# A top-k search on two engines: one engine's tiles given to the scheduler first, and a mask operation moved from ScalarE to VectorE

## The chip, the core and the metric

The kernel runs on one core of a Trainium2 chip. The core has five instruction streams that run side by side and in order: TensorE (PE, matrix products), VectorE (DVE), ScalarE (ACT), GpSimd (POOL) and SyncE (SP), which here only issues DMA transfers. The metric is the device time of one execution, in microseconds; lower is better.

## The reference, cut to what matters

One transformer layer over 1024 tokens of width 1024. After a norm, one projection of the input feeds four token mixers: a convolution (A), differential attention (B), stick-breaking attention (C) and sparse attention (D). Their results are gated, merged and projected, and a gated feed-forward layer follows. The part that matters here is the key selection of D:

```python
logits = einsum('bqhd,bkd->bqhk', qi[:, t0:t1], ki[:, :kl]) * IDX_HD ** -0.5
score = einsum('bqhk,bqh->bqk', relu(logits), wi[:, t0:t1])
score = where(arange(kl) <= qpos, score, -inf)
_, idx = top_k(score, 256)
...
s = einsum('bqhd,bqkd->bqhk', q[:, t0:t1], k[idx]) * scale
p = softmax(where(valid, s, -inf))
```

For each of the 1024 query rows the 256 best scored keys are kept, and the attention runs over these alone. The kernel does it with a mask: it finds the value of the 256th best score of each row, and adds 0 to the attention scores of the chosen keys and -1e30 to the others.

## The kernel before, in words

Rows are handled in tiles of 128 (`t` is 0 to 7; tile `t` has `(t+1)*128` keys). Tiles 0 and 1 have at most 256 keys and need no search. The scores of tiles 2 to 7 lie side by side in one SBUF tile, `score`; `sct(t)` is the part of tile `t`.

The 256th best value is found bit by bit, in two halves: 15 bits of the upper 16 bits of the score (into `T1`), then 16 bits of the lower half among the keys whose upper half is equal (into `T2`). In each round, each tile counts how many keys reach the trial value, and the bit is kept or not. VectorE does tiles 7, 6, 3 and 2 (`V_T`, `search_v`, lines 609 to 619): one count for each tile (L605, scratch output `junkb`) and three small operations on all four (L614, L617, L618). ScalarE does tiles 5 and 4 (`A_T`, `search_a`, lines 621 to 636): three operations for each tile and round (L632, L633, L634), and L636 at the end.

Between the halves lies a step on VectorE for every tile (lines 650 to 659): a count of the keys above `T1` (L605), a test for equality (L654, scratch output `eqb`), a product that puts the lower halves of the scores into the keys (L657). At its end the wanted rank `kreq` is lowered by the counts (L659), and from it ScalarE's search gets `kq` (L625, L626). After both halves, lines 662 to 666 join the halves into the value `Tx`, and lines 668 to 678 make the mask of each tile, `t` = 2 to 7: a count (L605), an equality (L672), a running sum (L673), a comparison (L675), an addition (L677), all on VectorE, and last the mask itself, on ScalarE:

```python
A.activation(sct(t), keyt(t), AF.Identity, scale=-NEG, bias=negc)
```

Attention D starts at line 684. It takes tile 7 first (line 697). Its first VectorE operation, L708, adds the mask `sct(7)` to the scores of the keys, which TensorE has made (L466).

The instructions are written in program order and given to a scheduler, which lays them out on a timeline that it estimates: on each engine, of the instructions that it takes to be ready, the one that stands first in the program goes first. What comes out is a fixed stream for each engine. On the chip an instruction that waits holds up all that stand behind it in its engine's stream.

A tile pool hands out its buffers by tag. The scratch outputs `junkb` and `eqb` of VectorE's part come from one pool, `radj`, with one buffer and one tag:

```python
with pool("rad", 1) as rad, pool("radj", 1) as radj, pool("rada", 1) as rada:
...
def count(dst, src, t, scal, op):
    j = radj.tile([P, S], BF, name="junkb", tag="j")
```

ScalarE's scratch (`junka`) has a pool of its own, `rada`.

Around the search stand projections, which come before it in the program. Each (`proj`, line 356) loads a weight tile by DMA (`wraw`, line 181), splits it into a rounded part on ScalarE (`whi`, L184) and a rest, mostly on GpSimd (`wlo`, L185), and multiplies it in 48 TensorE instructions (L365). Results leave through ScalarE (L524 for plain tiles; L534, L535 and GpSimd's L536 for `qc` and `kc`; L397, L398, L402, L406 and GpSimd's L403, L404, L405, L407 for tiles with rotary positions) and are stored by DMA in `qk_s`. The gate projections (`gate_tile`, line 542) come after all attention in the program. The products of the modulation (`adaps` L202, `adae` L211, `adac` L214) pass through ScalarE too.

Of the kernel before, what the change touches and what calls it, by code (L numbers as in the profile page):

```python
# [12 lines left out]
BF = mybir.dt.bfloat16  # L13
I32 = mybir.dt.int32
U16 = mybir.dt.uint16
I16 = mybir.dt.int16
AF = mybir.ActivationFunctionType
OP = mybir.AluOpType
# [4 lines left out]
S = 1024  # L23
D = 1024
P = 128
# [6 lines left out]
NEG = -1.0e30  # L32
# [62 lines left out]
V_T = [7, 6, 3, 2]  # L95
A_T = [5, 4]
NV = len(V_T)


def kc(t):  # L100

    return V_T.index(t) if t in V_T else NV + A_T.index(t)
# [10 lines left out]
def tile_hybrid_block(ctx, tc, x, pos, ada, pk, cst, w_in, w_br, w_out, w_up, w_dn, out):  # L113
# [6 lines left out]
    V, G, A, PE = nc.vector, nc.gpsimd, nc.scalar, nc.tensor  # L120
# [28 lines left out]
    epsc, halfpi, onec, negc = zcol[:, 0:1], zcol[:, 1:2], zcol[:, 2:3], zcol[:, 4:5]  # L149
# [119 lines left out]
    with ExitStack() as mix:  # L269
# [11 lines left out]
        with pool("xtp", 1) as xtp, pool("adp", 8) as adp:  # L281
# [4 lines left out]
            for t in range(NT):  # L286
                xt = adp.tile([P, D], F32, name="xt", tag="w")
                dma(xt, x[t * P:(t + 1) * P, :])
                if t == 0:
# [9 lines left out]
                                op0=OP.mult, op1=OP.add)  # L299
# [15 lines left out]
            for m in range(4):  # L315
                mod_affine(m, A1, B1, "g1", pmm, "mm", stp, "st", adp)
                for j in (2 * m, 2 * m + 1):
                    V.tensor_scalar(out=xT[:, j, :], in0=xT[:, j, :], scalar1=A1[:, j:j + 1],
                                    scalar2=B1[:, j:j + 1], op0=OP.mult, op1=OP.add)
                    A.copy(hH[:, j, :], xT[:, j, :])  # L320
                    V.tensor_tensor(out=hL[:, j, :], in0=xT[:, j, :], in1=hH[:, j, :].bitcast(F32),  # L321
                                    op=OP.subtract)
# [3 lines left out]
            for kind in ("inv16", "inv32"):  # L326
# [4 lines left out]
                                op0=OP.mult, op1=OP.add)  # L331
                V.tensor_scalar(out=kk, in0=kk, scalar1=MAGIC, scalar2=None, op0=OP.subtract)
                for c in (_C1, _C2, _C3):
                    V.scalar_tensor_tensor(out=ang, in0=kk, scalar=-float(c), in1=ang,
                                           op0=OP.mult, op1=OP.add)
                V.tensor_scalar(out=ang, in0=ang, scalar1=3.1415925, scalar2=-3.1415925,
                                op0=OP.min, op1=OP.max)
# [9 lines left out]
        for i in range(2):  # L347
            V.tensor_tensor(out=lamt, in0=pc("lam", 64 * i, 64 * i + 32), in1=pc("lam", 64 * i + 32, 64 * i + 64),
                            op=OP.mult)
# [105 lines left out]
        NB = NT - 2  # L455
        off = [0]
# [32 lines left out]
        with pool("scp", 1) as scp, ExitStack() as scx:  # L489
            score = scp.tile([P, NTOT], F32, name="score")  # L490
            sct = lambda t: score[:, off[t - 2]:off[t - 1]]
            with pool("iqk", 4) as iqk, pool("itm", 3) as itm:
# [5 lines left out]
                for h in range(8):  # L498
# [3 lines left out]
                    for t in range(2, NT):  # L502
                        n = (t + 1) * P
# [4 lines left out]
                        if h == 0:  # L508
                            V.tensor_scalar(out=sct(t), in0=tmp[:, :n], scalar1=wiT[:, t, h:h + 1],
                                            scalar2=zcol[:, 3:4], op0=OP.mult, op1=OP.add)  # L510
                        else:
                            V.scalar_tensor_tensor(out=sct(t), in0=tmp[:, :n], scalar=wiT[:, t, h:h + 1],
                                                   in1=sct(t), op0=OP.mult, op1=OP.add)
# [71 lines left out]
            with pool("rad", 1) as rad, pool("radj", 1) as radj, pool("rada", 1) as rada:  # L585
                key = rad.tile([P, NTOT], BF, name="key")
                keyt = lambda t: key[:, off[t - 2]:off[t - 1]]
                cnt = rad.tile([P, NB], F32, name="cnt")
                ge = rad.tile([P, NB], F32, name="ge")
                sg_ = rad.tile([P, NB], F32, name="sg_")  # L590
                kreq = rad.tile([P, NB], F32, name="kreq")
                Ti = rad.tile([P, 2, NB], I32, name="Ti")
                T1 = rad.tile([P, NB], F32, name="T1")
                T2 = rad.tile([P, NB], F32, name="T2")
# [7 lines left out]
                def count(dst, src, t, scal, op):  # L602
                    j = radj.tile([P, S], BF, name="junkb", tag="j")
                    n = (t + 1) * P
                    V.tensor_scalar(out=j[:, :n], in0=src, scalar1=scal, scalar2=None, op0=op, op1=OP.add,  # L605
                                    accum_out=dst[:, kc(t):kc(t) + 1])
                    return j

                def search_v(T, dt, bits):

                    v = slice(0, NV)
                    V.memset(T[:, v], 0.0)
                    for b in range(bits - 1, -1, -1):
                        V.tensor_scalar(out=cf[:, v], in0=T[:, v], scalar1=float(1 << b), scalar2=None, op0=OP.add)  # L614
                        for t in V_T:
                            count(cnt, keyt(t).bitcast(dt), t, cf[:, kc(t):kc(t) + 1], OP.is_ge)
                        V.tensor_tensor(out=ge[:, v], in0=cnt[:, v], in1=kreq[:, v], op=OP.is_ge)  # L617
                        V.scalar_tensor_tensor(out=T[:, v], in0=ge[:, v], scalar=float(1 << b), in1=T[:, v],  # L618
                                               op0=OP.mult, op1=OP.add)

                def search_a(T, dt, bits):

                    a = slice(NV, NB)
                    V.memset(Bn[:, a], 0.5 - float(1 << (bits - 1)))
                    V.tensor_tensor(out=kq[:, a], in0=pc("nn", NV), in1=kreq[:, a], op=OP.subtract)  # L625
                    V.tensor_tensor(out=kq[:, a], in0=kq[:, a], in1=kreq[:, a], op=OP.subtract)  # L626
                    for b in range(bits - 1, -1, -1):
                        for t in A_T:
                            k = slice(kc(t), kc(t) + 1)
                            n = (t + 1) * P  # L630
                            j = rada.tile([P, S], BF, name="junka", tag="j")
                            A.activation(j[:, :n], keyt(t).bitcast(dt), AF.Sign, bias=Bn[:, k], accum_out=sgs[:, k])  # L632
                            A.activation(sgn[:, k], sgs[:, k], AF.Sign, bias=kq[:, k])  # L633
                            A.activation(Bn[:, k], sgn[:, k], AF.Identity, bias=Bn[:, k],  # L634
                                         scale=-0.5 * float(1 << b))
                    A.activation(T[:, a], Bn[:, a], AF.Copy, scale=-1.0)  # L636
# [7 lines left out]
                for t in A_T + V_T:  # L644
                    c = off[t - 2]
                    V.tensor_scalar(out=keyt(t), in0=score.bitcast(BF)[:, 2 * c + 1:2 * off[t - 1]:2],
                                    scalar1=sg_[:, kc(t):kc(t) + 1], scalar2=None, op0=OP.mult)
                search_a(T1, I16, 15)
                search_v(T1, I16, 15)
                for t in A_T + V_T:  # L650
                    count(cnt, keyt(t).bitcast(I16), t, T1[:, kc(t):kc(t) + 1], OP.is_gt)
                    e = radj.tile([P, S], BF, name="eqb", tag="j")
                    n = (t + 1) * P
                    V.tensor_scalar(out=e[:, :n], in0=keyt(t).bitcast(I16), scalar1=T1[:, kc(t):kc(t) + 1],  # L654
                                    scalar2=None, op0=OP.is_equal)
                    c = off[t - 2]
                    V.tensor_tensor(out=keyt(t).bitcast(U16), in0=score.bitcast(U16)[:, 2 * c:2 * off[t - 1]:2],  # L657
                                    in1=e[:, :n], op=OP.mult)
                V.tensor_tensor(out=kreq, in0=kreq, in1=cnt, op=OP.subtract)  # L659
                search_a(T2, U16, 16)  # L660
                search_v(T2, U16, 16)
                V.tensor_copy(Ti[:, 0, :], T1)
                V.tensor_copy(Ti[:, 1, :], T2)
                V.scalar_tensor_tensor(out=Ti[:, 0, :], in0=Ti[:, 0, :], scalar=16, in1=Ti[:, 1, :],
# [3 lines left out]
                for t in range(2, NT):  # L668
                    n = (t + 1) * P
                    tx = Tx[:, kc(t):kc(t) + 1]  # L670
                    g_ = count(cnt, sct(t), t, tx, OP.is_gt)
                    V.tensor_scalar(out=keyt(t), in0=sct(t), scalar1=tx, scalar2=None, op0=OP.is_equal)  # L672
                    V.tensor_tensor_scan(out=sct(t), data0=ones[:, 0:1].to_broadcast([P, n]), data1=keyt(t),  # L673
                                         initial=cnt[:, kc(t):kc(t) + 1], op0=OP.mult, op1=OP.add)
                    V.scalar_tensor_tensor(out=keyt(t), in0=sct(t), scalar=float(TOPK), in1=keyt(t),  # L675
                                           op0=OP.is_le, op1=OP.mult)
                    V.tensor_tensor(out=keyt(t), in0=keyt(t), in1=g_[:, :n], op=OP.add)  # L677
                    A.activation(sct(t), keyt(t), AF.Identity, scale=-NEG, bias=negc)

            adx.close()  # L680

# [466 lines left out]
```

## Time and profile before

| | us |
|---|---|
| median of 3 runs | 2032.14 |
| lowest and highest run | 2029.38, 2036.47 |
| the profiled execution | 2032.69 |
| its span, first to last instruction | 2030.9 |
| busy in it: TensorE, VectorE, ScalarE, GpSimd | 1855.4, 1154.4, 829.5, 472.9 |

The rows in the section below come from the profiled execution; their times are in us from the start of its span. 1.8 us of its time lie outside the span. "Busy" counts instructions in execution; a matrix product that runs at a lower clock is busy for longer. "Granted clock" is the share of TensorE's full clock of 2.4 GHz that it was given; its lower level of 1.2 GHz reads as 0.5.

### The profile page before, as it was taken

The page shows a single profiled execution, that of the slowest core. Times are in us where ns is not written, and L with a number is a line of the kernel's source. Part 1 is how long each engine was busy: PE and PEld are TensorE (multiplying, and loading weights), DVE is VectorE, ACT ScalarE, POOL GpSimd, SP SyncE. Part 2 cuts the span into 40 slices and gives each one's busy share as a digit, 9 for nine tenths or more (in the row PEclk, how much of TensorE's full clock was granted, in tenths as well). Part 3 has the DMA queues.
Part 4 walks back from the last instruction along what each step waited for, and adds up shares of the span by engine and source line. Part 5 has one row for each costly group of instructions (what it writes and reads, how often), then busy time and mean ns, then how long its engine had stood idle before and what let it go on. Part 6 is the DMA issues. An engine that isn't in the chain of part 4 may idle for free. (4 is left out here: it accounts for less than half of the span.)

```text
span 2030.9 us, 22858 instructions
## 1 busy us (share of the span) xinstructions
PE 1855.4 (91%) x8792; PEld 1443.3 (71%) x8792; DVE 1154.4 (57%) x1731; ACT 829.5 (41%) x1458; POOL 472.9 (23%) x244
## 2 busy tenths in 40 slices
PE   6888877499999999899999899999999999999996
PEld 3655555376767776677787668788888888888875
DVE  6759999605899857685113765532343334433457
ACT  5556666236545645463222444333122212221122
POOL 0102145272111110011205610222122212222024
PEclk9988989699999999899999999999999999999999
DMA  8364423444514242513113632121111101111114
GB/s 312 94 165 151 174 84 93 126 92 104 187 57 125 78 129 69 147 42 115 62 63 129 225 122 83 63 73 42 32 63 58 47 32 52 62 52 42 32 62 145
DMA packets 61038, 197.30 MB, mean 97 GB/s; under 512 B 9153, under 2 KB 9281, under 8 KB 60929
## 3 DMA queue, kind: packets, MB, share of 16 engines
q1 hardware_dynamic: 60928, 195.84, 30.6%
q8 instruction: 69, 1.13, 0.2%
q14 instruction: 41, 0.33, 0.1%
HBM read 154.13 MB, written 41.68 MB: 96 GB/s over the span
## 5 line engine op out<-in xcount | busy, mean ns | idle before, releaser
L185 POOL TENSOR_TENSOR wlo<-wraw,whi 128x1024 fp32r<-128x1024 f32 x126 | 317.4, 2521 | 1384.2 <-ACT whi L184 1348.2
L365 PE MATMUL mm<-hH,whi 128*128 128x512 f32 x864 | 353.5, 409 | 49.6 <-ACT whi L184 31.5
L365 PE MATMUL mm<-hH,wlo 128*128 128x512 f32 x864 | 350.4, 406 | 3.7 <-POOL wlo L185 3.7
L365 PE MATMUL mm<-hL,whi 128*128 128x512 f32 x864 | 351.9, 407 | 0.9 <-DVE hL L321 0.9
L184 ACT CAST whi<-wraw 128x1024 fp32r<-128x1024 f32 x144 | 150.6, 1049 | 413.2 <-PE ups L1017 283.7
L1017 PE MATMUL ups<-h2h,whi 128*128 128x512 f32 x704 | 277.6, 395 | 1.3 <-DVE h2h L994 1.3
L1017 PE MATMUL ups<-h2l,whi 128*128 128x512 f32 x704 | 277.5, 394 | 0.5 <-DVE h2l L995 0.5
L1017 PE MATMUL ups<-h2h,wlo 128*128 128x512 f32 x704 | 274.5, 390 | 0.0
L1022 DVE SCALAR_TENSOR_TENSOR u<-ups,pkt,u 128x1023 f32<-128x1023 f32 x44 | 56.4, 1283 | 350.8 <-ACT u L1021 350.8
L365 PEld LDWEIGHTS mm<-hH,whi 128*128 128x128 f32 x864 | 166.6, 193 | 95.6 <-ACT whi L184 32.0
L365 PEld LDWEIGHTS mm<-hH,wlo 128*128 128x128 f32 x864 | 166.5, 193 | 41.4 <-POOL wlo L185 4.8
L365 PEld LDWEIGHTS mm<-hL,whi 128*128 128x128 f32 x864 | 167.2, 194 | 36.1 <-issue 2.6
L1017 PEld LDWEIGHTS ups<-h2h,whi 128*128 128x128 f32 x704 | 132.6, 188 | 32.3 <-DVE h2h L994 1.7
L1017 PEld LDWEIGHTS ups<-h2h,wlo 128*128 128x128 f32 x704 | 132.5, 188 | 29.8
L1017 PEld LDWEIGHTS ups<-h2l,whi 128*128 128x128 f32 x704 | 132.7, 189 | 28.2 <-DVE h2l L995 1.0
L1052 DVE TENSOR_TENSOR ya<-ya,dps 128x1024 f32<-128x1024 f32 x80 | 97.3, 1217 | 58.8 <-PE dps L1047 58.6
L605 DVE TENSOR_SCALAR_CACHE_REDUCE junkb<-key,cf 128x1024 bf16<-128x1024 uint16 (+3 forms) x124 | 117.3, 946 | 4.3
L1047 PE MATMUL dps<-whi,ah 128*128 128x512 f32 x352 | 109.4, 392 | 5.5 <-DVE ya L1052 5.5
L1047 PE MATMUL dps<-wlo,ah 128*128 128x512 f32 x352 | 108.6, 390 | 0.0
L1047 PE MATMUL dps<-whi,al 128*128 128x512 f32 x352 | 108.4, 389 | 0.0
L872 DVE SCALAR_TENSOR_TENSOR hc<-hpad,pkt,hc 128x1024 f32<-128x1024 f32 x60 | 84.2, 1408 | 0.0
L1047 PEld LDWEIGHTS dps<-whi,ah 128*128 128x128 f32 x352 | 65.4, 188 | 22.2 <-DVE ya L1052 8.9
(560 smaller groups left out, 2950.3 us busy)
## 6 DMA issues: line engine op xcount, KB each, us to landing
wraw<-in_w_in SPq DMA_DIRECT2D x54, 512.0 KB, 3.9
adaw<-in_ada SPq DMA_DIRECT2D x48, 512.0 KB, 5.9
wraw<-in_w_up SPq DMA_DIRECT2D x44, 512.0 KB, 3.3
sg_s<-gt SPq DMA_DIRECT2D x44, 256.0 KB, 2.6
sgl<-sg_s SPq DMA_DIRECT2D x22, 512.0 KB, 3.4
wraw<-in_w_dn SPq DMA_DIRECT2D x22, 512.0 KB, 3.3
xt<-in_x SPq DMA_DIRECT2D x16, 512.0 KB, 4.9
qis<-qk_s SPq DMA_DIRECT2D x16, 256.0 KB, 4.2
```

The costliest lines, as they stand in the source:

```text
L184: A.copy(hi, raw)
L185: (E or G).tensor_tensor(out=lo, in0=raw, in1=hi.bitcast(F32), op=OP.subtract)
L365: PE.matmul(ps, a[:, ks], b[:, k, cs], start=(n == 0), stop=(n == 3 * NK - 1))
L605: V.tensor_scalar(out=j[:, :n], in0=src, scalar1=scal, scalar2=None, op0=op, op1=OP.add, accum_out=dst[:, kc(t):kc(t) + 1])
L872: V.scalar_tensor_tensor(out=hc, in0=hpad[:, k:k + S], scalar=w(k), in1=hc, op0=OP.mult, op1=OP.add)
L1017: PE.matmul(ps[:, hf * 512:hf * 512 + 512], a[:, ks], b, start=(n == 0), stop=(n == 23))
L1022: V.scalar_tensor_tensor(out=u[:, 1:], in0=ps[:, 0:S - 1], scalar=w(1), in1=u[:, 1:], op0=OP.mult, op1=OP.add)
L1047: PE.matmul(ps[:, cs], a[:, tb], b[:, cs], start=(n == 0), stop=(n == tot - 1))
L1052: V.tensor_tensor(out=ya[t], in0=ya[t], in1=ps, op=OP.add)
```

## The change

Two edits. The search is written engine by engine: first ScalarE's two tiles through the first half, the step between the halves and the second half, then VectorE's four tiles the same way; the step between the halves and the lowering of `kreq` are done for each group of tiles on its own columns. The last operation of the mask moves from ScalarE to VectorE, as (key - 1) times 1e30.

```diff
-                search_a(T1, I16, 15)
-                search_v(T1, I16, 15)
-                for t in A_T + V_T:
-                    count(cnt, keyt(t).bitcast(I16), t, T1[:, kc(t):kc(t) + 1], OP.is_gt)
-                    e = radj.tile([P, S], BF, name="eqb", tag="j")
-                    n = (t + 1) * P
-                    V.tensor_scalar(out=e[:, :n], in0=keyt(t).bitcast(I16), scalar1=T1[:, kc(t):kc(t) + 1],
-                                    scalar2=None, op0=OP.is_equal)
-                    c = off[t - 2]
-                    V.tensor_tensor(out=keyt(t).bitcast(U16), in0=score.bitcast(U16)[:, 2 * c:2 * off[t - 1]:2],
-                                    in1=e[:, :n], op=OP.mult)
-                V.tensor_tensor(out=kreq, in0=kreq, in1=cnt, op=OP.subtract)
-                search_a(T2, U16, 16)
-                search_v(T2, U16, 16)
+                def second(tiles, cols):
+
+                    for t in tiles:
+                        count(cnt, keyt(t).bitcast(I16), t, T1[:, kc(t):kc(t) + 1], OP.is_gt)
+                        e = radj.tile([P, S], BF, name="eqb", tag="j")
+                        n = (t + 1) * P
+                        V.tensor_scalar(out=e[:, :n], in0=keyt(t).bitcast(I16), scalar1=T1[:, kc(t):kc(t) + 1],
+                                        scalar2=None, op0=OP.is_equal)
+                        c = off[t - 2]
+                        V.tensor_tensor(out=keyt(t).bitcast(U16), in0=score.bitcast(U16)[:, 2 * c:2 * off[t - 1]:2],
+                                        in1=e[:, :n], op=OP.mult)
+                    V.tensor_tensor(out=kreq[:, cols], in0=kreq[:, cols], in1=cnt[:, cols], op=OP.subtract)
+
+                for tiles, cols, search in ((A_T, slice(NV, NB), search_a), (V_T, slice(0, NV), search_v)):
+                    search(T1, I16, 15)
+                    second(tiles, cols)
+                    search(T2, U16, 16)
...
-                    A.activation(sct(t), keyt(t), AF.Identity, scale=-NEG, bias=negc)
+                    V.tensor_scalar(out=sct(t), in0=keyt(t), scalar1=1.0, scalar2=-NEG, op0=OP.subtract,
+                                    op1=OP.mult)
```

## Rows read from the trace of the kernel before

**Rows 1.** Windows: stretch, busy time of PE, PEld, DVE, ACT, POOL, granted clock, DMA share.

```profile
235.00:262.00 27.00, 10.07 (x52) 6.70 (x50) 25.70 (x64) 6.16 (x11) 1.48 (x1) 0.77 0.15 60
262.00:349.00 87.00, 76.36 (x322) 59.15 (x322) 83.34 (x174) 62.26 (x166) 49.37 (x38) 0.94 0.32 102
349.00:390.00 41.00, 6.84 (x18) 4.60 (x17) 38.43 (x58) 8.30 (x11) 8.96 (x4) 0.54 0.28 82
390.00:458.00 68.00, 64.22 (x279) 52.06 (x278) 0.00 (x0) 24.71 (x39) 47.52 (x33) 1.00 0.50 116
458.00:958.00 500.00, 472.29 (x2818) 354.74 (x2817) 376.03 (x641) 277.21 (x558) 71.67 (x31) 0.98 0.36 107
```

**Rows 2.** Waits in 150 to 470: total us, times, longest.

```profile
DVE pd L708 <- PE sc L466: 69.4, 1, 69.4
...
ACT score L678 <- DVE key L677: 33.4, 6, 11.9
...
PE mm L365 <- ACT whi L184: 31.5, 1, 31.5
...
PE adac L214 <- ACT adae L211: 25.3, 3, 16.9
```

**Rows 3.** ScalarE's timeline: start, duration, instruction, idle before and its releaser.

```profile
235.26 0.20 ACT L636 ACTIVATE T<-Bn 128x2 f32<-128x2 f32 x1
...
256.32 0.93 ACT L632 ACTIVATE junka<-key,Bn 128x768 bf16<-128x768 uint16 x1 [18.95 <-DVE key L657]
...
259.41 1.03 ACT L184 CAST whi<-wraw 128x1024 fp32r<-128x1024 f32 x1
...
360.71 0.58 ACT L534 ACTIVATE chi<-mm 128x512 fp32r<-128x512 f32 x1
...
379.93 1.98 ACT L184 CAST whi<-wraw 128x1024 fp32r<-128x1024 f32 x2
```

**Rows 4.** VectorE's timeline: first and last instructions of the search's stages.

```profile
181.50 1.27 DVE L605 TENSOR_SCALAR_CACHE_REDUCE junkb<-key,cf 128x1024 bf16<-128x1024 int16 x1
...
253.82 1.00 DVE L605 TENSOR_SCALAR_CACHE_REDUCE junkb<-key,T 128x768 bf16<-128x768 int16 x1
...
268.73 1.28 DVE L605 TENSOR_SCALAR_CACHE_REDUCE junkb<-key,cf 128x1024 bf16<-128x1024 uint16 x1
...
355.57 0.17 DVE L663 CAST Ti<-T 128x6 int32<-128x6 f32 x1
...
385.91 2.74 DVE L677 TENSOR_TENSOR key<-key,junkb 128x1024 bf16<-128x1024 bf16 x1
458.09 1.22 DVE L708 CUSTOM_DVE_ANT_0 pd<-sc,score 128x1024 f32<-128x1024 f32 x1 [69.44 <-PE sc L466]
```

**Rows 5.** SyncE's timeline: issues of DMA transfers.

```profile
364.36 1.65 SPq L123 DMA_DIRECT2D wraw<-in_w_in  x2
...
500.29 1.05 SPq L123 DMA_DIRECT2D vt<-v_s  x2
```

**Rows 6.** DMA issues in 300 to 400: KB each, median us to landing.

```profile
wraw<-in_w_in SPq DMA_DIRECT2D x5, 512.0 KB, 4.8
```

**Rows 7.** Groups by line in 172 to 390: busy us, mean ns, idle before.

```profile
L678 ACT ACTIVATE score<-key,zcol 128x384 f32<-128x384 bf16 (+5 forms) x6 | 5.3, 882 | 33.4 <-DVE key L677 33.4
...
L672 DVE TENSOR_SCALAR key<-score,Tx 128x384 bf16<-128x384 f32 (+5 forms) x6 | 3.4, 574 | 0.0
```

**Rows 8.** TensorE's timeline.

```profile
265.04 0.63 PE L365 MATMUL mm<-hH,wlo 128*128 128x512 f32 x1
...
541.80 0.22 PE L466 MATMUL sc<-kcs,qcs 128*128 128x128 f32 x1
...
547.82 1.09 PE L744 MATMUL tr<-ctile,vt 128*128 128x128 f32 x8
```

**Rows 9.** VectorE's timeline: one small operation of a search round.

```profile
303.36 3.71 DVE L618 SCALAR_TENSOR_TENSOR T<-ge,T 128x4 f32<-128x4 f32 x1
```

**Rows 10.** Windows, columns as in group 1, for 181 to 254.

```profile
181.00:254.00 73.00, 58.83 (x288) 43.23 (x288) 69.46 (x170) 48.03 (x139) 12.00 (x16) 0.90 0.49 173
```

## Prediction

> **What bounds the kernel now.** I read the windows by stage first [rows 1]. TensorE is busy for 472 of the 500 us after 458 and waits much in two stretches before that: 10.1 us busy in 235 to 262, and 6.8 in 349 to 390. VectorE is the reverse: full until 390, then without one instruction until 458. So TensorE's stream sets the end, and those two holes are what can be won.
>
> The waits name what ends them [rows 2]. TensorE waits 16.9 us at once for `adae` and 31.5 us for `whi`, both made by ScalarE; ScalarE waits 33.4 us in six pieces for the keys of its mask operation. VectorE waits 69.4 us, once, for the score products of attention D: today the mask is done 69 us before it can be used.
>
> ScalarE's stream shows why its work is late [rows 3]. It ends its first half at 235.46, but its second half stands next in its stream and gets its keys only at 256.32, after 18.95 us of waiting; `whi` and `adae` stand behind and come at 259.41 and later. The same from 349 on: behind mask operations that wait for VectorE stand L534 of the last `kc` half (360.71) and the two `whi` at 379.93. VectorE's own stages follow without a gap [rows 4]: first half 181.50 to 253.82, 72.3 us for 15 rounds, 4.82 each; the step between the halves to 268.73, 14.9; second half to 355.57, 86.8 for 16 rounds, 5.43 each; masks to 388.65, 33.1 (the last instruction starts at 385.91 and takes 2.74).
>
> **The mask operation.** ScalarE loses six operations that cost it 5.3 us and, with their waits, the hole from 349. Not all of the hole goes. The next weights were requested at 364.36 [rows 5], behind the stores of the tile that L534 gives out, so 3.65 us after L534 began; a weight tile lands 4.8 us after its issue [rows 6]; its rounding takes 1.05. That is 9.5 us, and 2.6 more which TensorE then waited for GpSimd's rest. So the hole shrinks from 34.2 (31.55 and 2.61) to about 12.1: 22.1 us for TensorE. Bounds: nothing, if the weights are what is late in any case, and all 34.2.
>
> VectorE gains six operations. The trace has none that reads these keys and writes f32. The nearest row is L672 on the same tiles, 3.4 us for six; the dearer bound is ScalarE's 5.3, the cheaper one nothing, if they fill gaps between dependent operations [rows 7]. I take 3.4, because L672 is the same kind of instruction on the same engine. The Trainium skill ("ScalarE: Activation LUTs", Rules for kernel authors) puts additions and multiplications on VectorE, up to about three times faster in bf16; the six would then cost 1.8 us and not 3.4, which nothing here decides.
>
> **The order of the search.** ScalarE's path gets short: its step between the halves no longer stands behind `search_v` in the program. If VectorE is free when ScalarE ends its first half at 235.46, the first keys come 2.5 us later (253.82 to 256.32 today) and TensorE's 16.9 us go.
>
> VectorE's path is the question: who may write the one scratch buffer of `radj`? The step of tiles 5 and 4 now stands ahead of all rounds of `search_v`, and both write that buffer. Whether buffers are handed out in program order can be read elsewhere in the trace. The `vt` loads were issued at 500.29 [rows 5], but their transposes ran at 547.82, only when attention D's transposes, which use the same tag and come earlier in the program, were over; a score product of C, later in the program and with another tag, ran before them at 541.80 [rows 8]. Program order by tag explains this; so it does that the step took tiles 5 and 4 ahead of VectorE's own. I take it to hold. Then VectorE can't start a round before ScalarE's first half is over and its two tiles are through: no instruction is added, but the 72.3 us that run beside ScalarE's first half move behind it. Queued behind in VectorE's stream are the copy of `vd`, the masks and L708, for which D waits.
>
> The sum for VectorE: 235.5 + 14.9 (both parts of the step) + 72.3 + 86.8 + 33.1 + 3.4 + 0.2 (one subtraction more) = 446.2.
>
> A second term comes on top. A round's small operations wait while GpSimd works: one of 0.16 us took 3.71 [rows 9]. The price by rows: the second half's rounds cost 0.61 more each than the first half's, 9.8 us for 16. GpSimd was busy 49.4 us under them (262 to 349, rows 1) against 12.0 under the first half [rows 10], some 12.8 for 16 rounds: 9.8 over 36.6 is 0.27 us lost per us of GpSimd. The 47.5 us of GpSimd work in 390 to 458, where VectorE now sleeps, would fall under its rounds: +12.8. The 12.0 under today's first half would meet an idle VectorE: -3.2. Bounds: no loss for the 47.5, or one for one. I take the row's rate: mask ready at 455.8.
>
> The Trainium skill ("SBUF — State Buffer", SBUF: two separate sides) speaks against the change here: VectorE operations with two SBUF inputs or in a two-port mode and GpSimd operations exclude each other for a whole instruction. At its hardest that is one for one, and a rival below; the trace shows 0.27.
>
> TensorE would have reached D at about 456.9 - 16.9 - 22.1 = 417.8 (456.9 is its start today, 1.2 before L708). Its products there are no longer what D waits for: VectorE is late next, L708 moves from 458.09 to 455.8, and 38 us of won time turn into a new wait. Gate products can't fill it, since they stand behind D's in TensorE's stream, as I expect the order to stay.
>
> After such a wait TensorE is cold: behind the first hole a product took 0.63 us [rows 8], and the granted clock of 349 to 390 was 0.54, the level of 1.2 GHz. At the upper level a product takes 0.23 (64.22 for 279, rows 1); some eight at half pace cost 1.8 us more. I put +2 on the path, bounds 0 and 4. The profiled execution is 2032.69 (0.55 above the median of the runs): 2032.69 - 2.3 + 2 = 2032.4, no change that counts.
>
> **The rivals.** (1) The scratch buffer does not bind, and the step of ScalarE's tiles lands on VectorE as soon as ScalarE is ready. VectorE's chain then stays as it is, ready by about 393, and TensorE sets the start of D: 2032.7 - 16.9 - 22.1 = 1993.7, or 1992 with a warm clock. For it: the names of the tiles are free of each other. Against: the `vt` rows.
>
> (2) The buffer does not bind, but the scheduler, from its own estimate, puts the step into VectorE's stream where it is now, behind the first half. The first hole stays and 22.1 is won: 2010.6. If its place is five rounds further, behind VectorE's own step, the first hole grows by 10 + 5 x 5.4 = 37: 2048.
>
> (3) Slower: GpSimd and VectorE exclude each other one for one. The mask is then ready at 446.2 + 47.5 - 3.2 = 490.5, and D starts 32.4 later: 2032.7 + 32.4 + 2 = 2067. It decides from a loss of 0.4 per us, where the gain is spent and 0.3% is passed. For it: the 3.71 us operation. Against: counts, most of a round, are not stretched.
>
> (4) The change doesn't do what it says: `whi` is late for its DMA and not for the mask. That is in the bounds of the 22.1, and with VectorE as the bound it changes nothing.
>
> **How the numbers follow.** No difference within 0.3% (6.1 us) can be told from no change. Forecast (VectorE sets the start of D): 0.72. Its own range is 2018 (no loss to GpSimd: start 443.0) to 2044 (a loss of 0.5); of it I put 0.17 faster, 0.35 same, 0.20 slower. Rival 1: 0.08. Rival 2: 0.10 at its near place, 0.05 at the far one. Rival 3: 0.05. Faster: 0.17 + 0.08 + 0.10 = 0.35. Same: 0.35. Slower: 0.20 + 0.05 + 0.05 = 0.30. The range 2006 to 2048 holds the forecast but for 0.02 and rival 2, and leaves out rivals 1 and 3: 0.15 out.
>
> **What would show it.** In the changed kernel: VectorE nearly idle from 182 to 235; `junka` of the second half within 5 us of L636; no hole of TensorE at 245; the hole after `kc` near 12 us; then a wait of TensorE of some 35 us before D's transposes, with VectorE full until L708 at about 456; and six new VectorE operations of about 0.6 us. What would make it wrong: VectorE's rounds running beside ScalarE's first half (rivals 1 and 2), gate products ahead of D, or a loss to GpSimd far from 0.27.

## The result and the profile after

The changed kernel takes 2046.03 us (median of 6 runs, 2040.46 to 2048.37) where the kernel before takes 2035.82 (6 runs beside it): ratio 1.0053, 95% interval 1.0033 to 1.0073. It is slower, by 10.2 us; 2032, no change, was forecast, with 2006 to 2048 as the range. (The profiled execution, 2040.46, is the shortest of the six; from the output projection on it is 1.3 to 3.0 us shorter than the other kernels profiled here. So places ahead of that are compared in what follows, not its end.)

The windows by stage of the changed kernel (columns as in group 1) show where the work went:

```profile
172.00:235.00 63.00, 59.51 (x291) 43.73 (x290) 11.15 (x33) 49.25 (x142) 11.99 (x16) 0.95 0.53 193
235.00:262.00 27.00, 26.45 (x138) 19.03 (x137) 25.85 (x60) 23.70 (x67) 5.49 (x6) 1.00 0.51 192
262.00:349.00 87.00, 72.82 (x296) 56.99 (x295) 83.58 (x161) 51.31 (x119) 55.47 (x38) 0.94 0.36 106
349.00:390.00 41.00, 40.04 (x176) 32.53 (x175) 39.28 (x78) 14.28 (x23) 28.80 (x20) 1.00 0.49 116
390.00:458.00 68.00, 16.12 (x66) 12.42 (x65) 62.85 (x124) 8.79 (x15) 13.96 (x11) 0.64 0.17 31
458.00:500.00 42.00, 21.20 (x156) 16.52 (x156) 18.43 (x46) 18.22 (x36) 12.14 (x8) 0.69 0.51 157
```

Both old holes of TensorE are filled: 26.5 us busy in 235 to 262 (10.1 before, [rows 1]) and 40.0 in 349 to 390 (6.8 before). By 390 it is some 50 us ahead. Then it does 16.1 us of work in 68 and 21.2 in 42. VectorE, full in 172 to 235 before, now sleeps there, and is full from 235 to 454.

The waits of the changed kernel in 150 to 520 (total, times, longest), to be held against [rows 2]:

```profile
POOL r L403 <- ACT r L402: 52.6, 1, 52.6
DVE junkb L605 <- ACT T L636: 51.6, 1, 51.6
ACT pd L721 <- DVE sm L720: 51.1, 4, 48.5
...
PE sc L466 <- DVE sm L712: 48.4, 1, 48.4
...
PE sc L466 <- DMA qds<-qk_s: 18.3, 1, 18.3
```

The first count of the step waits 51.6 us for ScalarE's first half. At the other end TensorE and ScalarE wait 48 us for D's first score operation, and GpSimd, behind a copy on ScalarE, 52.6. The last row was not forecast. The timeline of the changed kernel, rows of four engines put in order of time, shows where it comes from:

```profile
234.13 0.20 ACT L636 ACTIVATE T<-Bn 128x2 f32<-128x2 f32 x1
234.37 1.01 DVE L605 TENSOR_SCALAR_CACHE_REDUCE junkb<-key,T 128x768 bf16<-128x768 int16 x1 [51.63 <-ACT T L636]
236.87 0.94 ACT L632 ACTIVATE junka<-key,Bn 128x768 bf16<-128x768 uint16 x1 [0.63 <-DVE key L657]
...
404.73 1.29 PE L466 MATMUL sc<-kds,qds 128*128 128x512 f32 x5
...
453.17 1.23 DVE L712 CUSTOM_DVE_ANT_0 pd<-sc,score 128x1024 f32<-128x1024 f32 x1
454.62 1.15 ACT L721 ACTIVATE pd<-pd,sm 128x1024 f32<-128x1024 f32 x1 [48.50 <-DVE sm L720]
459.39 1.09 ACT L402 ACTIVATE r<-mm 128x512 f32<-128x512 f32 x2
465.67 3.54 SPq L123 DMA_DIRECT2D qk_s<-rhi  x8
469.62 3.61 SPq L123 DMA_DIRECT2D qk_s<-sw  x8
473.28 0.45 SPq L123 DMA_DIRECT2D qds<-qk_s  x1
473.77 0.58 SPq L123 DMA_DIRECT2D wraw<-in_w_in  x1
477.14 1.62 PE L466 MATMUL sc<-kds,qds 128*128 128x512 f32 x3 [18.26 <-DMA qds<-qk_s]
479.20 1.04 ACT L184 CAST whi<-wraw 128x1024 fp32r<-128x1024 f32 x1 [13.56 <-DMA wraw<-in_w_in]
```

It reads from 477.14 upwards. D's second head waits for a query load issued at 473.28. That load stands on SyncE's queue behind the stores of a rotated tile; the tile's copy (L402) stands on ScalarE behind D's first exponential (L721); and that waited for the mask. Before, all eight query loads were issued by 392.

The kernels were then compared by two places: D's first VectorE operation (L712 here, 458.09 before) and the first product of the mixers' output projection (L929 here, 974.70; L925 before, 964.00). The stretch between is 505.9 us before and 521.5 after. So the start of D is 4.9 us earlier, the stretch is 15.6 longer, and the sum, 10.7, is near the 10.2 between the medians. Windows of the gate products alone (L365: length, busy time and count of PE and PEld) split the stretch near the last transpose of attention B, the kernel before first:

```profile
458.00:917.00 459.00, 263.61 (x948) 171.79 (x948) 0.98 0.36 104
917.00:964.00 47.00, 38.53 (x157) 29.30 (x157) 1.00 0.36 118
```

The changed kernel:

```profile
453.00:917.00 464.00, 254.52 (x900) 161.34 (x900) 0.95 0.34 100
917.00:974.60 57.60, 49.10 (x205) 38.25 (x204) 1.00 0.33 115
```

Gate products fill TensorE beside the attention stages. The changed kernel does 900 of them there and 205 behind, before 948 and 157. The 48 take 48 x 0.23 = 11.0 us behind the attention, and the attention stages themselves 4.6 more. But both kernels do the same products, only at another place. Windows over the whole stretch (columns as in group 1), the kernel before first, show what is lost:

```profile
458.10:964.00 505.90, 478.19 (x2844) 359.55 (x2843) 381.98 (x642) 277.11 (x558) 71.67 (x31) 0.98 0.36 105
```

```profile
453.20:974.70 521.50, 478.13 (x2844) 360.33 (x2845) 380.54 (x642) 277.15 (x555) 67.85 (x30) 0.95 0.34 102
```

TensorE is busy for 478.2 and 478.1 us. So the 15.6 us are idle time, 27.7 before and 43.4 after, and the one wait of 18.3 us for the query load is more than the whole difference. The count tells that another order was written; the wait is what this order costs. The load is not alone: the next weights of the gate products stand right behind it on SyncE's queue (473.77) and are rounded only at 479.20. With the load by itself out of the way, TensorE would by these rows have waited for the weights instead; no run shows it.

### The profile page after: what moved, and what is told of

It is laid out like the page before. It is cut to its first block, busy times and chain, and to the rows that moved or that the text cites. A ratio compares the mean times of both kernels' runs of the same rounds, so it can differ in the third digit from the quotient of the medians.

```text
span 2038.6 us, 22872 instructions
## 1 busy us (share of the span) xinstructions
PE 1852.0 (91%) x8792; PEld 1440.5 (71%) x8792; DVE 1162.4 (57%) x1738; ACT 825.7 (41%) x1452; POOL 465.2 (23%) x244
## 5 line engine op out<-in xcount | busy, mean ns | idle before, releaser
L185 POOL TENSOR_TENSOR wlo<-wraw,whi 128x1024 fp32r<-128x1024 f32 x126 | 310.9, 2469 | 1378.3 <-ACT whi L184 1378.2
L365 PE MATMUL mm<-hH,whi 128*128 128x512 f32 x864 | 353.9, 410 | 22.6 <-ACT r L402 10.5
L365 PE MATMUL mm<-hL,whi 128*128 128x512 f32 x864 | 351.1, 407 | 1.2 <-DVE hL L321 1.2
L365 PE MATMUL mm<-hH,wlo 128*128 128x512 f32 x864 | 349.0, 404 | 2.0 <-POOL wlo L185 2.0
L365 PEld LDWEIGHTS mm<-hH,whi 128*128 128x128 f32 x864 | 166.6, 193 | 69.9 <-ACT r L402 12.6
L365 PEld LDWEIGHTS mm<-hH,wlo 128*128 128x128 f32 x864 | 166.0, 192 | 39.2 <-issue 3.3
L365 PEld LDWEIGHTS mm<-hL,whi 128*128 128x128 f32 x864 | 166.4, 193 | 35.2 <-issue 2.6
L1056 DVE TENSOR_TENSOR ya<-ya,dps 128x1024 f32<-128x1024 f32 x80 | 97.4, 1218 | 58.8 <-PE dps L1051 58.5
L605 DVE TENSOR_SCALAR_CACHE_REDUCE junkb<-key,cf 128x1024 bf16<-128x1024 uint16 (+3 forms) x124 | 117.2, 946 | 4.3
L466 PE MATMUL sc<-kds,qds 128*128 128x512 f32 (+3 forms) x96 | 27.1, 390 | 66.7 <-DVE sm L712 48.4
```

What stands on the lines that cost most here:

```text
L185: (E or G).tensor_tensor(out=lo, in0=raw, in1=hi.bitcast(F32), op=OP.subtract)
L365: PE.matmul(ps, a[:, ks], b[:, k, cs], start=(n == 0), stop=(n == 3 * NK - 1))
L466: PE.matmul(ps[:, c0:c1], a, b[:, c0:c1], start=(si == 0), stop=(si == len(stacks) - 1 and not last))
L1056: V.tensor_tensor(out=ya[t], in0=ya[t], in1=ps, op=OP.add)
```

## The experiments

Each ratio is to the kernel before, run on the same chip.

**One edit at a time (e1, e2).** The two edits taken apart:

```diff
 e1: old order of the search, and
-A.activation(sct(t), keyt(t), AF.Identity, scale=-NEG, bias=negc)
+V.tensor_scalar(out=sct(t), in0=keyt(t), scalar1=1.0, scalar2=-NEG, op0=OP.subtract, op1=OP.mult)
 e2: new order of the search, with the first of these two lines
```

> The kernel before with only the mask's last operation moved to VectorE; the search keeps its old order. My theory (the hole from 349 was ScalarE standing behind the mask operations, and the move by itself is a gain): VectorE's mask ready near 392, D free to start well before 458, hole 2 down from 34.2 to between 0 and 12.1, hole 1 of 16.9 stays: 22 to 34 us faster than before, ratio 0.983 to 0.989. Rival (the weights are late for another reason, or VectorE's operation costs as much as it saves): no change, ratio 0.998 to 1.002.

> The changed kernel with the mask's last operation back on ScalarE; only the order of the search is changed. My theory (the order alone carries the loss, since VectorE can't start its rounds before ScalarE's first half is over): VectorE idle from 182 to 234 as in the changed kernel, the first score operation of D at 450 to 455, ScalarE held behind mask operations instead of D's exponential, the time within 0.4% of the changed kernel, ratio to before 1.001 to 1.009. Rival (the two edits hurt only together): not slower than before, ratio under 1.000.

e1: 2012.98 us, ratio 0.9888 (0.9869 to 0.9907), as expected. Its waits in 172 to 620:

```profile
PE adac L214 <- ACT adae L211: 25.3, 3, 16.9
...
PE mm L365 <- ACT whi L184: 10.3, 1, 10.3
...
DVE pd L709 <- PE sc L466: 55.1, 6, 39.2
```

The 16.9 us hole is untouched, the 34.2 shrank to 11.9 (10.3 and, as before the change, a wait for GpSimd's rest, 1.6), and VectorE still has 39 us to spare before D.

e2: 2086.39 us, ratio 1.0241 (1.0222 to 1.0259). VectorE idles 51.5 us as the theory has it, but the expected time was far off. Its waits in 340 to 520:

```profile
ACT score L681 <- DVE key L680: 105.1, 6, 83.7
...
PE mm L365 <- ACT whi L184: 85.7, 1, 85.7
```

The mask operation stands in ScalarE's stream far ahead of the time when VectorE now delivers, and `whi` stands behind it. So the order alone costs 50 us, the mask operation alone gains 23, and with the new order its move is worth some 40 (2086.4 to 2046.0): it takes ScalarE's other work out from behind a wait that the new order had made longer.

**A scratch buffer of its own (e3).**

```diff
-def count(dst, src, t, scal, op):
-    j = radj.tile([P, S], BF, name="junkb", tag="j")
+def count(dst, src, t, scal, op, tag="j"):
+    j = radj.tile([P, S], BF, name="junkb", tag=tag)
...
+tag = "e" if tiles is A_T else "j"      # in second(), for both its scratch outputs
```

> The changed kernel with a scratch buffer of its own for the step of ScalarE's two tiles. Theory (the one buffer, handed out in program order, is what holds VectorE from 182 to 234): the 51.6 us wait on T is gone and the rounds start at 183. Where the step then lands is the planner's choice; in the written-out order it stands four rounds into VectorE's second half, so ScalarE waits from 235 to about 287 and TensorE's first hole comes back at about 45 us; ScalarE's second half ends near 370, mask ready near 405, D starts at 450 to 463: 2027 to 2039, ratio 0.995 to 1.002. Rival (the buffer binds nothing): VectorE still idle to 234, ratio as the changed kernel, 1.003 to 1.007.

2034.69 us, ratio 1.0000 (0.9989 to 1.0011), inside the range. Its waits in 172 to 470:

```profile
DVE pd L713 <- PE sc L466: 51.9, 1, 51.9
...
PE adac L214 <- ACT adae L211: 46.6, 2, 40.4
ACT junka L632 <- DVE key L658: 40.9, 1, 40.9
```

The wait of 51.6 us is gone with the shared buffer: the buffer was what bound VectorE. And the first hole is back at 40.4 us, since the scheduler put the step of ScalarE's tiles some three rounds into VectorE's second half (its `eqb` starts at 276.80, VectorE's own step ends at 261). This is the prediction's rival 2 near its far place, which was put at five rounds and 2048.

**The buffer's order used by hand (e5, e6, e7).** If the one buffer goes round in program order, the step can be written between two chosen rounds:

```diff
 e5 (k = 11; e6: k = 4; e7: k = 11, mask operation on ScalarE)
+search_a(T1, I16, 15)
+search_v(T1, I16, 15, None, 15 - k)        # the first k of the 15 rounds
+second(A_T, slice(NV, NB))
+search_a(T2, U16, 16)
+search_v(T1, I16, 15, 15 - k, 0)           # the other rounds
+second(V_T, slice(0, NV))
+search_v(T2, U16, 16)
```

> The changed kernel with the step of ScalarE's two tiles written after eleven of VectorE's fifteen rounds of the first half, so that the one scratch buffer's order lets these eleven rounds run beside ScalarE's first half. Theory (the buffer's order alone costs VectorE 51.6 us, and that is the 48.4 us wait of TensorE before D): VectorE waits at most 3 us for ScalarE near 235, no hole of TensorE at 245 or 349, mask ready near 400, TensorE reaches D near 405 without a wait; the 18.3 us for the eighth query load stays. About 48 us faster than the changed kernel: 1992 to 2002, ratio to before 0.979 to 0.984. Rival (the wait before D has another cause, such as GpSimd taking VectorE's time): mask ready after 420, ratio above 0.990.

> As the run before, with four rounds ahead of the step instead of eleven: a dose in between. Theory: VectorE waits 30 to 34 us for ScalarE instead of 51.6, mask ready near 434, TensorE's wait before D 27 to 31 us, the 18.3 us for the query load stays: 17 to 21 us faster than the changed kernel, ratio to before 0.994 to 0.997. Rival: time doesn't follow the rounds; ratio as the changed kernel or as the run with eleven.

> The run with eleven rounds, with the mask's last operation back on ScalarE. Theory (ScalarE's stream holds everything behind a mask operation that waits for VectorE): the hole at 245 is gone, ScalarE is held by the first mask operation from about 330 to 360, and TensorE has a hole of 30 to 45 us there instead: 10 to 20 us faster than before, ratio 0.990 to 0.995. Rival (once the order is right the place of the operation doesn't matter): as the run with eleven rounds, 0.979 to 0.984.

e6: 2036.66, ratio 1.0006 (0.9996 to 1.0017); e5: 2016.80, ratio 0.9909 (0.9895 to 0.9924). Both gained less than expected, and e5 lies where its rival was put: mask ready after 420, ratio above 0.990. VectorE's wait for ScalarE is 51.6 us with no round ahead, 31.4 with four, and no longer in the list with eleven; D's first score operation comes at 453.17, 443.05 and 424.54, TensorE's wait before it falls from 48.4 to 34.0 and 10.0. The dose works, but the start of D moves by only about half of it, since VectorE now meets more of GpSimd's work: the second half's rounds take 95 us in both (about 317 to 412, and 273 to 368) where the changed kernel's take 87.6, and in e5 the masks are stretched too. Windows over the masks alone (stretch, busy time of PE, PEld, DVE, ACT, POOL), of the changed kernel:

```profile
422.20:453.10 30.90, 0.00 (x0) 0.00 (x0) 30.05 (x45) 0.00 (x0) 0.00 (x0) 0.50 0.00 0
```

of e1:

```profile
357.30:400.50 43.20, 38.49 (x156) 30.67 (x157) 42.47 (x44) 10.18 (x16) 24.31 (x11) 0.90 0.61 168
```

and of e5:

```profile
369.80:424.50 54.70, 37.84 (x150) 29.54 (x149) 53.87 (x44) 16.88 (x27) 46.06 (x25) 0.90 0.38 73
```

The same operations take 30.9 us beside no GpSimd work, 43.2 beside 24.3 and 54.7 beside 46.1: about 0.5 us for each. In the first of these windows the other engines stand still too; e11, below, tells GpSimd's part from theirs. The 24 us between the first and the last are about what e5 missed of the 400 that were expected: the 8 us more of its second half are made up by its first half, which has 17.2 us of GpSimd beside it and not 50.7.

e7: 2054.84, ratio 1.0099 (1.0083 to 1.0114), a miss: 0.990 to 0.995 was expected. ScalarE waits 38.4 us at the first mask operation and TensorE 34.6 and 15.5 behind it, so D starts at 459.49, no earlier than before; and the stretch behind it is 526.9, with 237 gate products left behind the attention. The place of the mask operation does matter in either order.

**The load behind the stores (e4, e8, e9).** Three tries at the 18.3 us:

```diff
 e4: kds and all four query tiles of the first pair loaded ahead of the qc, kc, qb and kb projections
+kds = dqk.tile(...); dma(kds.bitcast(F32), ...)
+q0 = load_qd(0)
 for i in range(2):
     hl_tile("qc", i, 0.125)
...
 e8: no fourth tile
+if pr == 0 and len(qs) == 3:
+    q = qs[2]
...
 e9: the fourth tile alone loaded ahead
+q0 = {3: load_qd(0, 1, 1)}
 for i in range(2):
     hl_tile("qc", i, 0.125)
```

> The changed kernel with the loads of kds and of the first four query tiles of D written ahead of the qc, kc, qb and kb projections, so that they are issued before those tiles' stores. Theory (the second hole of 18.3 us comes from the eighth query load standing on SyncE's queue behind the stores of a rotated tile whose work stood on ScalarE behind D's first exponential): that hole goes, the wait of 48 us before D stays, 14 to 18 us faster than the changed kernel, ratio to before 0.995 to 0.999. Rival (something else is late at 477 too, such as weights or the keys): the hole is renamed and the time stays, ratio 1.003 to 1.007.

> The changed kernel without its fourth query tile's load (the seventh and eighth issue): the third tile is used in its place, so these scores are others, and all work on the engines stays, with D at the same place in the streams. Theory (TensorE's second wait, 18.3 us, is only for the load that stands on SyncE's queue behind stores that stand behind ScalarE's held stream): that wait goes, the 48 us before D stay, 14 to 18 us faster than the changed kernel, ratio to before 0.996 to 0.999. Rival (weights or another late product take its place): ratio 1.003 to 1.007.

> The changed kernel with the load of D's fourth query tile alone written ahead of the qc projections. In the written-out streams this puts both heads' products of D together again, as before, and leaves 589 gate products behind the last transpose of attention B, as in the kernel before, where the changed kernel has 637. Theory (mask ready at 453 is not what made the changed kernel slower; the other order behind D is: the 18 us for the fourth tile and 48 gate products that no longer run beside the attention stages): the wait of about 48 us before D stays, the 18 us wait goes, and the stretch from D's first score operation to the first output product is 505 to 508 us as before, not 521: ratio to before 0.996 to 0.999, 2028 to 2033. Rival (the late start of D, its cold clock and ScalarE's held stream cost it): the stretch stays near 521, ratio 1.003 to 1.007.

e4: 2088.92, ratio 1.0260 (1.0243 to 1.0278), far off. With all loads early the scheduler put D's products ahead of the `qb` and `kb` projections, where they wait for the same mask, in TensorE's timeline:

```profile
342.04 2.00 PE L466 MATMUL sc<-kds,qds 128*128 128x512 f32 x8
443.69 4.70 PE L466 MATMUL sc<-kds,qds 128*128 128x512 f32 x12 [99.65 <-DVE sm L718]
```

The projections that had covered 50 us of the wait now stood behind it.

e8, which uses the third tile in place of the fourth: 2053.72, ratio 1.0088 (1.0073 to 1.0103), another miss. The 18 us wait is gone and the kernel is slower still. Its gate products beside the attention:

```profile
455.00:920.80 465.80, 244.10 (x868) 157.57 (x869) 0.95 0.33 97
```

and its whole stretch:

```profile
455.70:985.90 530.20, 487.63 (x2840) 364.55 (x2841) 384.26 (x642) 276.76 (x555) 72.72 (x30) 0.95 0.33 99
```

Without the load the scheduler wrote a third order behind D. In it TensorE idles 42.6 us, in waits of 5.7 at most, and is busy 9.5 us longer than in the changed kernel. So e8 does not tell what the load costs where the order is kept: it changed both.

e9 puts the load where the order behind D becomes that of before: 2031.99, ratio 0.9992 (0.9981 to 1.0003). Its wait before D (150 to 620), its gate products beside the attention and its whole stretch:

```profile
PE sc L466 <- DVE sm L721: 45.7, 4, 43.7
```

```profile
457.00:919.50 462.50, 263.60 (x948) 171.99 (x948) 0.97 0.34 101
```

```profile
457.50:966.40 508.90, 480.54 (x2840) 361.90 (x2841) 382.26 (x642) 275.54 (x554) 69.22 (x29) 0.97 0.35 103
```

D starts at 457.51 after a wait of 43.7 us, with a granted clock that had fallen to 0.50 (426.9 to 457.5) and with ScalarE held 45.0 us by the same exponential, and yet the stretch behind it is 508.9, with 28.4 us of idle TensorE, and the time that of before. So the wait, the fallen clock and the held ScalarE are not by themselves what made the changed kernel slower; the order written behind D is, with the late transfers in it. The load and the order changed together here too. All profiled kernels but e4 fall into three groups, by the products beside the attention (one is missing from some traces): 948, stretch 505.1 to 508.9, TensorE idle for 27.6 to 28.4 us of it (before, e1, e3, e9, e10, e11); 900, 521.5 to 524.7, idle 42.7 to 45.7, each with a wait of 18.0 to 19.3 for the late load (changed, e2, e5, e6); 868, 526.9 and 530.2, idle 41.1 and 42.6, without that wait and with 7.5 to 9.4 us more of busy time than before (e7, e8).

**Both repairs (e10), and less work for GpSimd (e11).** e10 is e5 with e9's load. e11 leaves out the rotation of `qb` and `kb`:

```diff
+if name not in ("qb", "kb"):
     E.tensor_tensor(out=r[:, cs], in0=r[:, cs], in1=cs_t[:, cs], op=OP.mult)
     E.tensor_tensor(out=sw[:, cs], in0=sw[:, cs], in1=sn_t[:, cs], op=OP.mult)
     E.tensor_tensor(out=r[:, cs], in0=r[:, cs], in1=sw[:, cs], op=OP.add)
```

> The run with eleven rounds, with the same early load of the fourth tile. Theory: D's first score operation near 424.5 as in the run with eleven rounds, 505 to 508 us from there to the first output product: 32 to 35 us faster than before, ratio 0.982 to 0.985, and faster than either kernel and than the run with the mask operation alone (0.989). Rival: the order behind D costs nothing, and the time is that of the run with eleven rounds, 0.989 to 0.993.

> The run before this one without the rotation of qb and kb: three of the four operations that GpSimd does for each half of these four tiles (L403, L404, L405) are left out, so that these tiles are not rotated; matrix products, loads, stores and ScalarE's work stay. Theory (VectorE's mask operations are stretched by GpSimd, about 0.5 us for each us of GpSimd work beside them, by 30.9 us with none, 43.2 with 24.3 and 54.7 with 46.1): GpSimd has under 22 us beside the masks, the masks take 33 to 43 us instead of about 55, are ready by 412, and TensorE doesn't wait for them before D: 8 to 14 us faster than the run with the rotation. Rival (the stretch comes from TensorE or ScalarE using the same memory, or from DMA): the masks still take 50 us or more.

e10: 2004.82 us, ratio 0.9852 (0.9833 to 0.9871), 28 us faster than before by the medians (32 to 35 were expected) and the fastest whole kernel here. D starts at 429.28 and the stretch is 507.7. One reading of the expectation was wrong: VectorE is no longer what D waits for. Its mask is done at 415.9, and it waits in its timeline

```profile
429.28 1.23 DVE L726 CUSTOM_DVE_ANT_0 pd<-sc,score 128x1024 f32<-128x1024 f32 x1 [13.37 <-DMA qk_s<-rhi]
```

for TensorE, which lost 18.8 us before it to copies of rotated tiles (L402). (The row names a transfer; TensorE's own product for it began at 428.15.)

e11: 1989.04, ratio 0.9782 (0.9761 to 0.9802), 14 us faster than e10 by the ratios and 16 by the medians, as much as was expected or more, but not in the expected way. GpSimd has 23.0 us beside the masks, and these take 45.2, not 33 to 43. D starts 14.8 earlier, for the most part because TensorE's waits for L402 fell from 18.8 to 6.7 us. The stretch of the masks stays with GpSimd's work, here at (45.2 - 30.9) / 23.0 = 0.62. It is not TensorE's, which is busy beside all of these masks: the running sum of the tile with 896 keys (397.57) overlaps no GpSimd instruction and takes 2.08 us, as in the changed kernel (2.09); that of the tile with 1024 keys (403.33) overlaps GpSimd and takes 4.56 instead of 2.35.

## Why the prediction was wrong

**The scratch buffer: right.** VectorE can't begin until ScalarE's first half is over (51.6 us at L605), and the second half of ScalarE restarts 2.7 us after L636, as forecast. e3 shows that the buffer is the reason, e5 and e6 that its order in the program is.

**VectorE's sum: right, in part by luck.** 455.8 was forecast for the mask, 453.2 measured. Its terms: the first half of VectorE's rounds (with the copy of `vd`, 1.4) took 85.9 us and not 72.3, the second 87.6 and not 86.8, together 4.8 more than forecast with the 9.6 for GpSimd; the masks with the new operation took 30.9 and not 36.5, since no GpSimd work lay beside them. The two errors cancel. A round without GpSimd takes 4.56; the two halves lost 16 and 15 us beside 50.7 and 50.0 us of GpSimd, 0.32 and 0.29 per us, where 0.27 was taken from the rows. The rule of the Trainium skill ("SBUF — State Buffer", SBUF: two separate sides), read at its hardest as one for one, is not reached in the rounds; in the masks of the runs half of it is, or a little more.

**The mask operation: right in size.** Six operations, 3.2 us, from the groups by line of the changed kernel:

```profile
L681 DVE TENSOR_SCALAR score<-key 128x384 f32<-128x384 bf16 (+5 forms) x6 | 3.2, 526 | 0.2
```

3.4 was taken. Against ScalarE's 5.3 [rows 7] that is 1.7 times faster; the estimate of 1.8 us by the Trainium skill ("ScalarE: Activation LUTs", Rules for kernel authors) is not met; its figure is for bf16, and this operation reads bf16 and writes f32. Alone the move gains 23 us by the medians (22.1 was forecast), with a hole of 11.9 left over (12.1).

**The hole behind `kc`: wrong, without effect.** No 12 us are left in the changed kernel; its weights are requested at 344.82 and 362.35, in time. TensorE reached D at 404.73 and not 417.8, and so waited 48.4 us and not 38.

**The stretch behind D's start: the step that failed.** The sum was 2032.7 - 2.3 + 2, and it took the stretch from D's first operation to the end as it was; the only reason given is "as I expect the order to stay", said of the gate products. The term was 0 (2 with the cold clock) and measured 15.6. TensorE's busy time in the stretch is that of before (478.1 and 478.2 us), so the 2 for the clock does not show; its idle time went from 27.7 to 43.4 us, 18.3 of it in one wait for a query load that the new order put behind the stores of a rotated tile. Where the order became that of before, in e9, the idle time is 28.4 us and the time 2031.99, near the forecast. The text named what is queued on VectorE behind the new wait, and not what is queued on ScalarE and SyncE. A walk along these streams of before would have met half of it: the copy L402 stands behind D's exponentials there too (469.09), but all eight query loads are ahead of its stores. The late load belongs to the new order.

**What stays open.** Why the scheduler writes another order behind D when the search is reordered: the order of the streams can be read, the estimates that made it can't. And what the new order would cost without the late transfers: each run that moved the load or left it out (e4, e8, e9) also changed the order.

**The rivals.** Rival 1 (both holes go) is what e10 comes nearest to, with the order chosen by hand. Rival 2 comes nearest in e3. Rival 3 (one for one) did not happen.

## What to carry to other kernels

A buffer that is handed out in program order is a lock between engines: writing a loop engine by engine moves the lock, and a written-out interleaving (here eleven rounds, then the step) uses it. Where a wait moves, walk every stream that stands behind it, and don't carry the length of a later stage over from the trace of before when a scheduler writes the order: count the filler products beside the stage (948, 900, 868 here) to see whether the order changed, and compare the idle time of the engine that sets the pace (28, 43, 43 us) to see what that costs. An operation that waits in a busy engine's stream is worth moving for what stands behind it: the same move gained 23 us in one order and 40 in the other.

## What the runs showed of the hardware

GpSimd and VectorE slow each other, and by kind of work. Search rounds, mostly counts, lose about 0.3 us per us of GpSimd work in the changed kernel, and 0.4 in the second half of e5 and e6 (95 us beside 57.3 and 58.5, against 16 x 4.56); the mask operations lose 0.5 to 0.6. It goes both ways, as a group of GpSimd beside e5's masks shows (busy us, mean ns):

```profile
L405 POOL TENSOR_TENSOR r<-r,sw 128x512 f32<-128x512 f32 x5 | 9.4, 1883 | 0.4
```

The same L405 took 1.29 us in the changed kernel at 388.43, beside search rounds. So rotated tiles come later, and TensorE with them: its waits for L402 in 150 to 520 are 10.5 us in the changed kernel and 14.6 in e5.
